# Modulation by quarters of the features, and six projections of layer one summed between them

## The chip, the cores and the metric

The kernel runs on one core of a Trainium2 chip. The metric is the device time of one execution in microseconds. Five engines work side by side and meet at semaphores: TensorE (matmuls into psum, which has eight banks of 128x512 fp32 here), VectorE, ACT (ScalarE), GpSimd (POOL) and SyncE (SP), which only issues transfers. All transfers of this kernel are issued by SP, in order, and are carried by 16 DMA engines.

## The reference

A block of two layers over 256 tokens and 256 context tokens with 1024 features, and behind it two more layers of another kind. Only the beginning of the first layer matters here:

```python
silu_c, silu_cc = jax.nn.silu(c), jax.nn.silu(c_ctx)
for l in range(DEPTH):
    mod = silu_c @ mod_w[l] + mod_b[l]          # 3 x 1024: shift, scale, gate
    mod_c = silu_cc @ mod_w[l] + mod_b[l]
    x, xc = trunk_layer(x, xc, mod, mod_c, ...)

# trunk_layer
shift, scale, gate = jnp.split(mod[:, None, :], 3, axis=-1)
z = split_columns((rmsnorm(x, pre_g) * (1 + scale) + shift) @ w_in)
zc = split_columns((rmsnorm(xc, pre_g) * (1 + scale_c) + shift_c) @ w_in)
```

The columns of z that appear below are mla_q (256, "q"), mla_kv (128, "kv"), mla_kr with the two small gate ranks ("misc"), pool_x and pool_gate (512 each, "px" and "pg"). q and kv are normalised and feed an attention of eight heads; px and pg feed a pooling branch; both end in a merge.

## The kernel before

**Tiles.** Activations lie with features on the partitions: xn holds the normalised, modulated input as 8 blocks of 128 features by 512 tokens (context in columns 0 to 255, x in 256 to 511). Each value is kept as two parts, h (rounded to float32r) and l (the rest), written by `split` (L382: a cast on ACT, a subtraction on VectorE). Weights come in chunks of 128x1024 fp32, loaded by `raw` (L357, the transfer is L361) and split by `W_` (L368: the cast L377 on ACT, the subtraction L379 on VectorE, or on GpSimd for every second chunk while `lopool[0]` is 2). `mm3` (L391) makes three float32r matmuls for each block of 128 features: h by h, h by l, l by h (L395 to L397). A product of one chunk with xn (`ws`, L399) is 8 blocks by 3, 24 matmuls into one bank. wp is the pool of the weights, with three raw buffers, three for h and three for l.

**The start (L1111 to L1144).** Four token tiles are loaded (L1117), with the constants and the vectors (L1119, L1121). Each is scaled by its reciprocal norm (L1128, L1129) and transposed by TensorE (L1133) into xT. `mod_cols` (L473) then computes shift and scale: for each of four groups of 512 columns `mod_rows` (L458) loads four chunks of the modulation weights and makes 16 small matmuls (L466, eight records in the trace for each chunk, 32 output rows at a time), copies the bank (L470), transposes it (L479), reduces it to columns (L482) and adds the bias (L483; L486 for the scale). The groups come in the order 0, 2, 1, 3: shift and scale of the first half of the features, then of the second. After each half, xT is scaled and shifted in place (L1142, two token groups for each of four blocks) and split into xn (L1144). The raw modulation chunks lie in a pool "bd" with 16 buffers, which also holds xT and is closed after the start.

**Layer one (L634, called from L1168).** `latents` (L644) makes the products q 0, q 1, kv and misc by `win` (L640), takes squares for their norms, splits the scaled latents, sums the squares by one-column matmuls (L669, L671), takes reciprocal roots on GpSimd, spreads them by transposes (L445, L680, L683) and multiplies two loaded tables by them (L687, L688). `mla` (L697) then makes the values (uv), keys (uk) and queries (uq) of the heads from the split latents; the first scores are L735. `poolb` (L978) makes px g and pg g for four groups g. `trunk_core` (L1088) weaves these generators: for each step of the attention, a fraction of a step of the pooling and merging branch, and 0.7 of a step of the second layer's modulation (`mod_cols(1, md1)`, L1169). The tiles of latents, mla and poolb come from a pool "mla0" (L1091) that is opened after "bd" is closed.

**The order.** The program order gives priorities; a scheduler with a time model writes each engine's instructions in a fixed order from them before the run. On the chip each engine keeps that order and waits at semaphores. `ahead[0]` gives weights a higher priority from the latents on. Psum banks have three tags: "mm" with three, "at" with three, "aux" with two (L299 to L306). A product or a transpose holds its bank until it has been read.

## Time and profile before

| what | us |
|---|---|
| median of three runs | 1570.56 (1567.63 to 1571.66) |
| the profiled execution, its own time | 1570.03 |
| its span | 1568.3 |
| TensorE busy in it | 1492.4 |
| VectorE, ACT, GpSimd busy | 949.9, 756.1, 360.9 |
| transfers | 229.79 MB |

The profile is of one execution. Busy time of TensorE is from modelled ends, so that a busy TensorE need not be at its peak. [...] In rows of the trace a line names the line of the code, which may be that of a helper; "xna" is the first half of xn, "xnb" the second; PEld is TensorE's loading of weights, which overlaps its matmuls.

### The profile page before, as it was taken

What the parts mean: (1) busy time and instruction counts of PE and PEld (TensorE: products, weight loads), DVE (VectorE), ACT (ScalarE), POOL (GpSimd) and SP (SyncE); (2) the same over time, 40 slices, a digit from 0 to 9 for tenths busy, and PEclk for the clock granted to TensorE, in tenths of its full rate; (3) what the DMA queues carried; (4) which work ended last, traced back from release to release, by engine and by line L of the source; (5) the groups of instructions that cost most, each with busy time, mean ns of one, the idle gap of its engine ahead of it and who ended that gap; (6) DMA issues with size and microseconds to landing.
All of it is one profiled execution on the core that took longest, in us unless ns stands there. A gap on an engine that the chain in (4) does not pass through costs nothing.

```text
span 1568.3 us, 25530 instructions
## 1 busy us (share of the span) xinstructions
PE 1492.4 (95%) x10206; PEld 1284.0 (82%) x10206; DVE 949.9 (61%) x1479; ACT 756.1 (48%) x1267; POOL 360.9 (23%) x276
## 2 busy tenths in 40 slices
PE   6999999999999999998989989989999997899998
PEld 3766668787877789777889989869999887799986
DVE  5555435856445576667694764767665577656654
ACT  4444344453323365755644454554444457534443
POOL 1213125735400002336582020311000034100000
PEclk9999999999999999999999999999999999899999
DMA  8323322222334465224337664425556654435564
GB/s 340 121 103 125 121 90 81 66 76 68 108 110 163 144 189 168 95 74 137 104 133 254 196 217 145 132 85 169 165 186 187 217 187 148 140 130 179 185 187 135
DMA packets 65638, 229.79 MB, mean 147 GB/s; under 512 B 7280, under 2 KB 7920, under 8 KB 65392
## 3 DMA queue, kind: packets, MB, share of 16 engines
q1 hardware_dynamic: 65520, 228.16, 44.9%
q8 instruction: 80, 1.31, 0.3%
q14 instruction: 38, 0.31, 0.1%
HBM read 227.09 MB, written 1.05 MB: 145 GB/s over the span
## 4 chain that ended last, share of the span: by engine, by line
PE 77%; DVE 7%; POOL 4%; issue 4%; DMA 4%; ACT 4%; SPq 0%; POOLq 0%; DVEq 0%; ACTq 0%
PE mm L395 21%; PE mm L397 21%; PE mm L396 21%; DMA wr<-in_w_dram 3%; PE at L735 2%; DVE wl L379 2%; PE aux L768 2%; ACT wh L377 1%; PE at L755 1%; POOL wl L379 1%; POOL E L915 1%; POOL qp L895 1%; PE mm L466 1%; PE at L859 1%; PE aux L466 1%
## 5 line engine op out<-in xcount | busy, mean ns | idle before, releaser
L377 ACT ACTIVATE wh<-wr 128x1024 fp32r<-128x1024 f32 x352 | 370.8, 1055 | 424.9 <-PE mm L396 133.5
L379 DVE TENSOR_TENSOR wl<-wr,wh 128x1024 fp32r<-128x1024 f32 x288 | 363.9, 1265 | 287.2 <-ACT wh L377 285.9
L395 PE MATMUL mm<-xnah,wh 128*128 128x256 f32 (+1 forms) x1192 | 367.9, 309 | 11.2 <-DVE rt L1452 10.3
L397 PE MATMUL mm<-xnah,wl 128*128 128x256 f32 (+1 forms) x1192 | 361.9, 304 | 3.0 <-DVE wl L379 2.1
L396 PE MATMUL mm<-xnal,wh 128*128 128x256 f32 (+1 forms) x1192 | 362.0, 304 | 0.2 <-DVE xnal L386 0.2
L395 PEld LDWEIGHTS mm<-xnah,wh 128*128 128x128 f32 x1192 | 226.6, 190 | 27.8 <-DVE rt L1452 10.6
L379 POOL TENSOR_TENSOR wl<-wr,wh 128x1024 fp32r<-128x1024 f32 (+1 forms) x64 | 158.3, 2473 | 353.3 <-ACT wh L377 268.8
L397 PEld LDWEIGHTS mm<-xnah,wl 128*128 128x128 f32 x1192 | 226.6, 190 | 14.9 <-DVE wl L379 2.7
L396 PEld LDWEIGHTS mm<-xnal,wh 128*128 128x128 f32 x1192 | 226.8, 190 | 10.1 <-issue 1.4
L419 POOL TENSOR_TENSOR sm<-sm,minus_half 128x1 f32<-128x1 f32 (+3 forms) x34 | 25.5, 751 | 628.7 <-DVE sm L567 356.3
L395 PE MATMUL mm<-xnbh,wh 128*128 128x512 f32 (+1 forms) x392 | 138.2, 353 | 0.0
L397 PE MATMUL mm<-xnbh,wl 128*128 128x512 f32 (+1 forms) x392 | 136.9, 350 | 0.0
L396 PE MATMUL mm<-xnbl,wh 128*128 128x512 f32 (+1 forms) x392 | 136.7, 349 | 0.0
L395 PE MATMUL mm<-wh,xnah 128*128 128x256 f32 x288 | 84.3, 294 | 8.5 <-ACT xnah L385 6.3
L395 PEld LDWEIGHTS mm<-xnbh,wh 128*128 128x128 f32 x392 | 75.6, 193 | 11.8 <-issue 2.5
L397 PEld LDWEIGHTS mm<-xnbh,wl 128*128 128x128 f32 x392 | 75.6, 193 | 11.2 <-issue 2.4
L396 PEld LDWEIGHTS mm<-xnbl,wh 128*128 128x128 f32 x392 | 75.7, 193 | 11.0 <-issue 2.1
L396 PE MATMUL mm<-wl,xnah 128*128 128x256 f32 x288 | 83.3, 291 | 1.1 <-POOL wl L379 1.1
L397 PE MATMUL mm<-wh,xnal 128*128 128x256 f32 x288 | 82.6, 290 | 0.7 <-DVE xnal L386 0.7
L396 PE MATMUL mm<-wl,hh 128*128 128x512 f32 x176 | 68.8, 391 | 0.0
L397 PE MATMUL mm<-wh,hl 128*128 128x512 f32 x176 | 68.8, 391 | 0.0
L395 PE MATMUL mm<-yh,wh 128*128 128x512 f32 (+1 forms) x192 | 65.6, 342 | 0.9 <-ACT scr L1030 0.9
(365 smaller groups left out, 2895.5 us busy)
## 6 DMA issues: line engine op xcount, KB each, us to landing
wr<-in_w_dram SPq DMA_DIRECT2D x398, 512.0 KB, 3.6
wr<-in_w_dram SPq DMA_DIRECT2D x18, 256.0 KB, 2.7
row<-in_rows_dram SPq DMA_DIRECT2D x8, 512.0 KB, 5.4
xt<-in_xin_dram SPq DMA_DIRECT2D x4, 512.0 KB, 5.8
scr<-in_rows_dram SPq DMA_DIRECT2D x8, 256.0 KB, 4.8
xr<-in_xin_dram SPq DMA_DIRECT2D x2, 512.0 KB, 4.7
xc<-in_xin_dram SPq DMA_DIRECT2D x2, 512.0 KB, 4.7
toep<-in_toep_dram SPq DMA_DIRECT2D x1, 1024.0 KB, 7.0
```

The source lines that it names most:

```text
L377: S.activation(ch.h, r, AF.Copy)
L379: eng.tensor_tensor(ch.l, r, ch.h.bitcast(F32), op=OP.subtract)
L395: T.matmul(dst, lh, rh, start=first and i == 0, stop=False)
L396: T.matmul(dst, lh, rl, start=False, stop=False)
L397: T.matmul(dst, ll, rh, start=False, stop=last and i == n - 1)
L419: G.tensor_tensor(y, m, minus_half[:, :n], op=OP.pow)
L466: T.matmul(p[32 * j:32 * j + 32, c0:c0 + 256], sc[:, k * 32:k * 32 + 32], r[:, j, :], start=half == 0, stop=half == 1, tile_position=(0, 3 ...
L735: T.matmul(pa[:, :n], qxs[pr, j][:, c0 + qt * P:c0 + qt * P + P], kxs[pr, j][:, :n], start=True, stop=True)
L755: T.transpose(pa[:, k * 256 + qt * P:k * 256 + qt * P + P], r[qt][:, (2 * k2 + k) * P:(2 * k2 + k + 1) * P], ident)
L768: T.matmul(py[64 * j:64 * j + 64, c0:c0 + 256], v[:, k, h * 64:h * 64 + 64], pTs[j][k // 2][:, k % 2, :], start=k == 0, stop=k == nk - 1, ...
L859: T.matmul(pa[c * s:c * s + s, t * 2 * s:(t + 1) * 2 * s], k_[:, i:i + s], q_[:, :, j:j + s], start=True, stop=True, tile_position=(0, c * s))
L895: (V, G)[j].tensor_tensor(b[r, j, :], gq[r], e[r], op=OP.mult)
```

## The change

`mod_cols` goes by quarters of the features: each of its four groups now holds 256 columns of the shift and the 256 of the scale that belong to them, so that after each group two blocks of features can be finished. It yields once more in each quarter. For the first layer its bank comes from "aux" and its raw chunks from 12 buffers.

In the start, the weights of six products (q 0, q 1 with the first quarter; kv, misc with the second; px 0, pg 0 with the third) are loaded behind the modulation chunks of that quarter, into the same 12 buffers, and split; h and l of the first three lie in wp, those of the last three in a new pool "early". After each quarter, its two blocks of xn are written and every product that has its weights takes the matmuls of these two blocks (and of all earlier blocks when it has just come). Each product has one bank that stays open from its first block to its last: three "mm", three "at". `win` later returns the finished bank instead of making the product. Transfers of weights from the latents on are queued on SP behind the last of these chunks until `begun[0]` is cleared.

```diff
+EARLY = [[("q", 0), ("q", 1)], [("kv", 0), ("misc", 0)], [("px", 0), ("pg", 0)], []]
+MODBUFS = 12
...
     def raw(key, pl=wp, bufs=3, width=CW):
...
-        nc.sync.dma_start(t[:, :n], w[INDEX[key]][:, :n])
+        with tc.issue_after(begun[0]) if begun[0] is not None else nullcontext():
+            begun[1] = nc.sync.dma_start(t[:, :n], w[INDEX[key]][:, :n])
...
-    def W_(key, pl, bufs):
-        r = raw(key)
+    def W_(key, pl, bufs, *where):
+        r = raw(key, *where)
...
-    def mod_rows(l, cb2, ptile, *where):
+    def mod_rows(l, cbs, ptile, *where):
+
         p = ptile()
-        for cb in (2 * cb2, 2 * cb2 + 1):
-            c0 = (cb % 2) * 256
+        for n, cb in enumerate(cbs):
+            c0 = n * 256
...
-    def mod_cols(l, md, *where):
-        md.col = const.tile([P, 16, 2], F32, name=f"mcol{l}")
-        for cb2 in (0, 2, 1, 3):
-            mr = yield from mod_rows(l, cb2, mmps, *where)
+    def mod_cols(l, md, ptile, *where):
+
+        col = const.tile([P, 4, 2, 2, 2], F32, name=f"mcol{l}")
+        md.shift = lambda kk, m: col[:, kk // 2, 0, kk % 2, m:m + 1]
+        md.scale = lambda kk, m: col[:, kk // 2, 1, kk % 2, m:m + 1]
+        for q in range(4):
+            mr = yield from mod_rows(l, (q, 4 + q), ptile, *where)
             pc = auxps()
             for j in range(4):
                 T.transpose(pc[:, j * P:(j + 1) * P], mr[:, j * P:(j + 1) * P], ident)
-            cl = md.col[:, 4 * cb2:4 * cb2 + 4, :]
-            bias = VC(("shift_b", l), 4 * cb2, 4) if cb2 < 2 else VC(("scale_b", l), 4 * cb2 - 8, 4)
+            cl = col[:, q].rearrange("p a k r -> p (a k) r")
             V.tensor_reduce(cl, pc.rearrange("p (j g r) -> p j r g", j=4, g=4)[:, :, 0:2, :], axis=AX.X, op=OP.add)
-            V.tensor_tensor(cl, cl, bias[:, :, None].to_broadcast([P, 4, 2]), op=OP.add)
-            if cb2 >= 2:
-                pre = VC(("pre", l), 4 * cb2 - 8, 4)
-                V.scalar_tensor_tensor(cl, cl, 1.0, pre[:, :, None].to_broadcast([P, 4, 2]), op0=OP.add, op1=OP.mult)
-        yield
+            for i, name in enumerate(("shift_b", "scale_b")):
+                bias = VC((name, l), 2 * q, 2)
+                V.tensor_tensor(col[:, q, i], col[:, q, i], bias[:, :, None].to_broadcast([P, 2, 2]), op=OP.add)
+            pre = VC(("pre", l), 2 * q, 2)
+            V.scalar_tensor_tensor(col[:, q, 1], col[:, q, 1], 1.0, pre[:, :, None].to_broadcast([P, 2, 2]), op0=OP.add, op1=OP.mult)
+            yield
...
         def win(name, i, t0=T0, t1=512):
+            if (name, i) in M.ready:
+                return M.ready.pop((name, i))[:, :t1 - t0]
             return ws(W(("win", l, name, i)), xn, t0, t1)
...
             weaves(M.latents(mp), (fill, 0.3))
+            begun[0] = None
...
-        mc = mod_cols(0, md0, bd, 16)
-        for half in range(2):
-            for _ in range(9 if half == 0 else 8):
+
+        ep = mkpool(st, "early")
+        mc = mod_cols(0, md0, auxps, bd, MODBUFS)
+        chs = []
+        for q in range(4):
+            for _ in range(5):
                 next(mc, None)
-            for k in range(4 * half, 4 * half + 4):
+            for key in EARLY[q]:
+                n = len(chs)
+                where = (wp if n < 3 else ep, 3)
+                ch = W_(("win", 0, *key), *where, bd, MODBUFS)
+                chs.append((key, ch, (mmps if n < 3 else atps)()))
+            for k in (2 * q, 2 * q + 1):
                 for g in range(2):
                     gs = slice(g * 256, g * 256 + 256)
...
+                    V.tensor_scalar(xT[:, k, gs], xT[:, k, gs], md0.scale(k, 1 - g), md0.shift(k, 1 - g), op0=OP.mult, op1=OP.add)
                 split(xn, (ALL, k), xT[:, k, :])
+            for key, ch, d in chs:
+                k0 = 0 if key in EARLY[q] else 2 * q
+                mm3(d, [(ch.h[:, k, :], ch.l[:, k, :], xn.h[:, k, :], xn.l[:, k, :]) for k in range(k0, 2 * q + 2)],
+                    k0 == 0, q == 3)
+        M0.ready.update({key: d for key, _, d in chs})
...
     trunk_layer(0, md0, xn, M0)
-    trunk_core(0, M0, mod_cols(1, md1))
+    begun[0] = begun[1].ins
+    trunk_core(0, M0, mod_cols(1, md1, mmps))
```

## Rows read from the trace of the kernel before

**Rows 1.** The page: busy us, share of the span, instructions of each engine.
```profile
PE 1492.4 (95%) x10206; PEld 1284.0 (82%) x10206; DVE 949.9 (61%) x1479; ACT 756.1 (48%) x1267; POOL 360.9 (23%) x276
```
**Rows 2.** Stretches: length, busy time by engine, granted clock, DMA share, GB/s.
```profile
12.00:20.30 8.30, 7.20 (x76) 4.01 (x68) 6.25 (x31) 4.08 (x9) 0.55 (x1) 1.00 1.02 409
20.30:28.00 7.70, 3.78 (x44) 1.21 (x44) 6.01 (x18) 2.52 (x4) 0.00 (x0) 0.99 1.03 407
28.00:32.00 4.00, 3.84 (x32) 1.46 (x36) 1.64 (x5) 0.00 (x0) 0.00 (x0) 0.60 1.03 410
32.00:41.00 9.00, 7.28 (x36) 4.85 (x29) 7.67 (x14) 5.66 (x7) 2.40 (x1) 1.00 0.48 161
...
58.00:62.00 4.00, 4.00 (x12) 3.10 (x12) 0.83 (x3) 0.27 (x1) 2.00 (x2) 0.57 0.49 150
...
77.60:157.00 79.40, 79.40 (x405) 54.75 (x401) 44.77 (x98) 35.90 (x76) 17.93 (x14) 1.00 0.33 113
```
**Rows 3.** In order of time, TensorE: start, length, instruction, idle before and releaser.
```profile
16.47 1.07 PE L466 MATMUL mm<-wr,sc 128*32 128x256 f32 x16
...
21.65 0.64 PE L466 MATMUL mm<-wr,sc 128*32 128x256 f32 x8 [0.64 <-DMA wr<-in_w_dram]
...
31.80 0.16 PEld L466 LDWEIGHTS mm<-wr,sc 128*32 128x32 f32 x8 [0.36 <-DMA wr<-in_w_dram]
...
33.25 0.66 PE L479 MATMUL aux<-ct,scr 128*128 128x128 f32 x4 [0.81 <-DVE scr L470]
```
**Rows 4.** In order of time: the chain from the modulation to the first products.
```profile
23.54 2.67 DVE L1142 TENSOR_SCALAR xT<-xT,mcol 128x256 f32<-128x256 f32 x8
...
32.51 0.69 DVE L470 COPY scr<-mm 128x512 f32<-128x512 f32 x1 [0.73 <-PE mm L466]
...
35.45 2.40 POOL L379 TENSOR_TENSOR wl<-wr,wh 128x1024 fp32r<-128x1024 f32 x1 [21.14 <-ACT wh L377]
...
35.59 4.68 DVE L1142 TENSOR_SCALAR xT<-xT,mcol 128x256 f32<-128x256 f32 x8
...
39.10 0.50 PE L395 MATMUL mm<-xnbh,wh 128*128 128x512 f32 x1
```
**Rows 5.** The tile xT: scalings, ns at least/median/most.
```profile
L1142 DVE TENSOR_SCALAR xT<-xT,mcol x16: 400/406/2409, 23.5 to 39.9; 128x256 f32<-128x256 f32 x16
```
**Rows 6.** In order of time: cast and subtraction of a weight chunk.
```profile
33.06 1.06 ACT L377 ACTIVATE wh<-wr 128x1024 fp32r<-128x1024 f32 x1 [6.18 <-DMA wr<-in_w_dram]
...
34.26 1.22 DVE L379 TENSOR_TENSOR wl<-wr,wh 128x1024 fp32r<-128x1024 f32 x1
```
**Rows 7.** In order of time, TensorE: matmuls of a product; first one on latents.
```profile
48.34 0.39 PE L396 MATMUL mm<-xnal,wh 128*128 128x512 f32 x1
48.58 0.40 PE L397 MATMUL mm<-xnah,wl 128*128 128x512 f32 x1
...
69.42 0.39 PE L395 MATMUL mm<-wh,kvnh 128*128 128x512 f32 x1
```
**Rows 8.** In order of time, TensorE: the norms' small matmuls, and the first scores.
```profile
54.19 1.62 PE L669 MATMUL aux<-ct,scr 128*128 128x1 f32 x14
...
56.87 1.05 PE L671 MATMUL aux<-ct,scr 128*128 128x1 f32 x8 [0.49 <-ACT scr L661]
...
66.20 1.03 PE L445 MATMUL aux<-ct,sm 128*128 128x128 f32 x8
...
77.55 1.13 PE L735 MATMUL at<-kx,qx 128*128 128x256 f32 x4
```
**Rows 9.** The last splits of xT, and what waited for them (last row: SP's waits).
```profile
41.32 2.49 DVE L386 TENSOR_TENSOR xnbl<-xT,xnbh 128x512 fp32r<-128x512 f32 x4
...
43.89 0.63 ACT L385 ACTIVATE pwh<-wr 128x512 fp32r<-128x512 f32 x1 [2.96 <-DVE xnbl L386]
...
44.56 0.69 DVE L386 TENSOR_TENSOR pwl<-wr,pwh 128x512 fp32r<-128x512 f32 x1 [0.75 <-ACT pwh L385]
...
SPq L687 <- DVE xnbl L386: 2.0, 1, 2.0
```

More of the change, by code (lines that the diff above doesn't have):

```diff
@@ L1 @@
-from contextlib import ExitStack
+from contextlib import ExitStack, nullcontext
 import numpy as np
@@ L355, in trunk_and_stack @@
     lopool = [0]
+    begun = [None, None]
     def raw(key, pl=wp, bufs=3, width=CW):
@@ L493, in mod_gates @@
         for c in range(2):
-            mr = yield from mod_rows(l, 4 + c, auxps, *where)
+            mr = yield from mod_rows(l, (8 + 2 * c, 9 + 2 * c), auxps, *where)
             bB, pB = rowhalf(("mod_b", l), c), rowhalf(("post", l), c)
@@ L536, in prenorm_trunk @@
                 sl = slice(k * 256, k * 256 + 256)
-                scale, shift = md.col[:, 8 + kk, m:m + 1], md.col[:, kk, m:m + 1]
+                scale, shift = md.scale(kk, m), md.shift(kk, m)
                 if k == 0:
@@ L1107, in trunk_and_stack @@
     md0, md1, M0, M1 = Obj(), Obj(), Obj(), Obj()
+    M0.ready, M1.ready = {}, {}
     right = ctx.enter_context(ExitStack())
@@ L1134, in trunk_and_stack @@
                 S.activation(xT[:, 4 * k4:4 * k4 + 4, t * P:t * P + P], p.rearrange("p (k t) -> p k t", k=4), AF.Copy)
-        mc = mod_cols(0, md0, bd, 16)
-        for half in range(2):
-            for _ in range(9 if half == 0 else 8):
-                next(mc, None)
-            for k in range(4 * half, 4 * half + 4):
+        ep = mkpool(st, "early")
[3 more added lines that the diff above has]
+            for _ in range(5):
+                next(mc, None)
+            for key in EARLY[q]:
[4 more added lines that the diff above has]
+            for k in (2 * q, 2 * q + 1):
                 for g in range(2):
                     gs = slice(g * 256, g * 256 + 256)
-                    V.tensor_scalar(xT[:, k, gs], xT[:, k, gs], md0.col[:, 8 + k, 1 - g:2 - g], md0.col[:, k, 1 - g:2 - g],
-                                    op0=OP.mult, op1=OP.add)
+                    V.tensor_scalar(xT[:, k, gs], xT[:, k, gs], md0.scale(k, 1 - g), md0.shift(k, 1 - g), op0=OP.mult, op1=OP.add)
                 split(xn, (ALL, k), xT[:, k, :])
+            for key, ch, d in chs:
[3 more added lines that the diff above has]
+        M0.ready.update({key: d for key, _, d in chs})
     lam = VC("lam")
```

## The prediction, made before the changed kernel was run

> **What bounds the kernel now.** I read the page's row of engines, then the stretches of the beginning with busy time and granted clock, then the beginning in order of time. TensorE is busy for 95% of the span [rows 1], and from 77.60 to 157 it is busy for 79.40 of 79.40 us at full clock [rows 2]: in that stretch there is no idle time to fill, so what TensorE does earlier shortens it. Idle time is left at the start. [...] Over that whole start the transfers run at 407 to 410 GB/s with the DMA engines full [rows 2]. So the start is bound by transfers: a chunk of 128x1024 fp32 (0.524 MB) takes 0.524/407 = 1.28 us, TensorE needs 0.64 us for its eight matmul records, and the last of the sixteen chunks of shift and scale is in at 31.80 [rows 3]. Behind that stands a fixed chain before a product can use the new features: the copy, four transposes (0.66 us), the reduction and biases, eight scalings, the splits [rows 3, 4].
>
> **The DMA order.** Six chunks of the first layer's weights (q 0, q 1, kv, misc, px 0, pg 0) move in front of the last modulation chunk. No byte is added. Counted back from 31.80, chunk slot n is in at 31.80 - 1.28 x (16 - n). The last modulation chunk of quarter 1 is slot 4 (16.4), of quarter 2 slot 10 (24.1), of quarter 3 slot 16 (31.8), of quarter 4 slot 22 (39.5): the modulation ends 7.7 us later than before. Fewer buffers (12 for 16) cost nothing by this order, as slot 13 reuses what slot 1 filled some 15 us earlier; without that cover one chunk of 1.28 us would be late.
>
> **The chain of a quarter.** Before, the second half took 39.10 - 31.80 = 7.3 us from its last chunk to the first product on the new features [rows 3, 4]. Its eight scalings took 4.68 us where those of the first half took 2.67, because one of them lasted 2.41 us beside GpSimd's subtraction of 2.40 us [rows 4, 5]. In the changed part the six subtractions are all on VectorE (the counter that gives every second one to GpSimd is still 0), so that those 2.0 us go. I take 5.0 us a quarter (bounds: 4 and 7.3), so new features are there at 21.4, 29.1, 36.8 and 44.5. VectorE has the load for it: four chains of some 4.0 us (0.7 copy, 4 scalings at 2.67/8, two splits at 2.49/4, and 0.7 as an estimate for four small ones [rows 4, 9]), six subtractions of 1.22 us [rows 6] and the small operations, at most the 6.25 us that it was busy from 12.00 to 20.30 [rows 2], are 30 us in the 32 us from 12 to 44: full, but in front. ACT's six more casts of 1.06 us [rows 6] have more room still. One more bias operation in each quarter is 0.2 us of its chain, inside the 5.0.
>
> **TensorE.** A product's matmul takes 0.235 us in a stream (48.34 to 48.58) [rows 7]; a product has 24, so 5.6 us, six 33.8. By quarters they are 12, 36, 60 and 36 matmuls: 2.8, 8.5, 14.1 and 8.5 us. A quarter of modulation is four chunks at 1.07/2 us [rows 3] and the transposes, 2.8 us. Quarter 1 of the products runs from 21.4 to 24.2 and then waits for features until 29.1. From there TensorE has work in hand: 29.1 + 8.5 + 2.8 = 40.4, + 14.1 + 2.8 = 57.3, + 8.5 = 65.8. At 65.8 all six products are closed. Before, five of them and 3.7 us of small matmuls (1.62 + 1.05 + 1.03) [rows 8] were done when the first product on the normalised latents started at 69.42 [rows 7]. Six products without the small ones would have been done at 69.42 - 3.7 + 5.6 = 71.3. The gross gain is **5.5 us**.
>
> **What is given back: the pool.** The tiles of the attention stage lie in a pool on the memory of the start's pools. Before, the first write to it on ACT and the first load into it on SP both waited until the last split of xT ended at 43.8, though they have nothing to do with xT [rows 9]: a pool is handed over when its last user is done. The change puts a second pool there, for the weights of misc, px 0 and pg 0, whose last reader is the last matmul of pg 0, at 65.8. So the split latents, the tables and the pool weights wait for that end, where before they were written from 43.9 on. After it come three casts on ACT (0.63 each) and one subtraction (0.69) [rows 9] before a latents product can start, 2.7 us with gaps. Part of the 3.7 us of small matmuls, whose inputs lie elsewhere, fills it. Bounds 0 and 2.7 us; I take **1.5**. Two of the three raw buffers (pool weights, uk) stay taken until then too, and SP's queue stands behind them; the uv weights have the third and come through, so I cost that at nothing. If uv were queued behind, its transfer and casts, 1.28 + 1.06 + 1.22 = 3.6 us at the least [rows 6], would be bare.
>
> **The clock.** The lower level came in 28 to 32 after a stretch with TensorE half idle, and again in 58 to 62 in a stretch of one-column matmuls [rows 2, 8]. The first cost little then, as TensorE waited for chunks; now products would run in it. The second cost 4 x 0.43 = 1.7 us. The new start may lose 1.7 us at 29 and be spared those at 58, or have both. Bounds -1.7 and +1.7; I take **0.8** lost.
> [...]
>
> **Psum and later work.** The six open sums hold six banks (three "mm", three "at") until read; the transposes of x use "at" too, but come before all of them. The first score matmul comes at 77.55 [rows 8], later than any of the six is read but pg 0's; if that one stayed, the scores would have two banks for three. I cost it at nothing, at most 2 us. The second layer's modulation has the same matmuls, one operation more per quarter on engines that are not the bound, and three of its twenty steps now come after the attention stage: nothing, at most 0.5 us. The order the scheduler writes for the rest of layer one can shift by a microsecond or two either way.
>
> **Sum.** 5.5 - 1.5 - 0.8 = 3.2 us less. The profiled execution took 1570.03 us (span 1568.3), so 1566.8; the median of the runs, 1570.56, stands 0.5 above it. I predict **1567.0**. About 0.3% (4.7 us) is what a measurement here tells from no change, so the forecast itself is in "the same".
>
> **Rivals.**
> First, *the whole gain*: the small matmuls cover the pool's hand-over, and the denser TensorE stream is spared the low clock at 58. Then 5.5 to 7.2 us go: 1570.0 - 6.4 = 1563.6. For it: 3.7 us of cover against 2.7 of chain. Against it: the first writers all waited for the pool in the trace [rows 9].
> Second, *the score chain sets the pace*, and it ends slower. pg 0 moves in front of the latents, so the scores come later: 65.8 + 3.7 + 1.5, then 8.1 us from the first latents product to the first scores as before (69.42 to 77.55) [rows 7, 8], is 79.1, 1.6 us later. TensorE gets its 5.6 us back only if the attention stage is bound by TensorE. If it is bound by its own chain, the delay stays: 1.6, with the 0.8 of the clock and up to 3.6 for weights that wait behind the pool, 1572 to 1576; 1574.5 as one value. It decides when the first scores come after 82. Against it: 79.40 of 79.40 us busy [rows 2]; but a busy TensorE in this profile is not one at its peak.
> [...]
> Fourth, *the products do not come between*: TensorE's queue is in order, and if it holds the open sums behind later modulation chunks they start at 39.5 + 0.6 and end at 40.1 + 33.8 = 73.9 instead of 71.3, slower by 2.6 and the pool's 1.5: 1574.1. Before, products and modulation chunks were hardly mixed, so the trace says little.
>
> **How the numbers follow.** The forecast (0.44) and the third rival (0.10) are within 0.3%, but for some 0.08 of the forecast's spread beyond 1565.9; the whole gain has 0.29; the score chain 0.11, of which 0.03 stays within; the products not between 0.06, half within. That is faster 0.37, the same 0.52, slower 0.11; as the order of all of layer one is written anew, and the bounds of the small items lean to loss, I move 0.05 from the same to slower. Range 1561.5 to 1574.5: from the whole gain with a little more to the slower rivals' values.
>
> **What would show it.** Right: the last modulation matmul near 39.5; products of q 0 by 22; TensorE busy from 29 to 66 nearly without a break; pg 0's last matmul at 64 to 69; then ACT's and VectorE's splits waiting for that matmul, and latents products 1 to 3 us behind. Wrong: splits of the latents written before pg 0 ends (no hand-over, whole gain); TensorE idle by 3 us or more between 29 and 60 waiting for modulation chunks (fourth rival); first scores after 82, or idle TensorE in the attention stage (second); a clock of 0.5 in 21 to 33 (third).

## The result, and the profile after

The changed kernel takes **1578.24 us** (median of 11 runs, 1573.73 to 1582.66) where the kernel before takes 1569.78 in the same session (11 runs, 1565.77 to 1573.29): a ratio of **1.0057**, 95% interval 1.0042 to 1.0072. It is slower by 0.57%. The forecast was 1567.0 with a range to 1574.5, so the prediction fell on the wrong side. The profiled execution took 1573.86 us (span 1571.9), at the low end of its runs. The ratios leave out a single slow execution, one of the twelve of e11, which took 2930.69 us.

The page's row of engines first, the counterpart of [rows 1]:

```profile
PE 1491.0 (95%) x10206; PEld 1281.9 (82%) x10206; DVE 955.5 (61%) x1494; ACT 755.7 (48%) x1267; POOL 352.1 (22%) x273
```

As many matmuls, and TensorE's busy time the same within 0.1%. So nothing was added to the bound engine: it stands idle, or works at the lower clock, somewhere that it did not before. The stretches of the changed kernel show where (columns as in [rows 2]: length, busy time by engine, granted clock, DMA share, GB/s). The granted clock is a share of full speed; read in slices of 0.5 us it is 1.00 or 0.50 all through 12 to 90, in both kernels, but for the slices in which it changes:

```profile
12.00:20.30 8.30, 6.04 (x63) 3.24 (x55) 6.46 (x27) 5.72 (x11) 0.54 (x1) 0.99 1.03 410
20.30:28.00 7.70, 5.98 (x26) 3.15 (x27) 6.98 (x19) 3.33 (x4) 0.00 (x0) 0.56 1.03 408
28.00:32.00 4.00, 4.00 (x23) 2.67 (x22) 0.69 (x1) 0.00 (x0) 0.00 (x0) 1.00 1.03 409
32.00:41.00 9.00, 8.68 (x66) 6.32 (x64) 8.01 (x22) 3.90 (x6) 0.00 (x0) 1.00 0.85 333
41.00:62.00 21.00, 18.01 (x98) 13.01 (x97) 4.33 (x12) 1.58 (x3) 0.00 (x0) 0.98 0.00 1
62.00:77.00 15.00, 14.29 (x65) 11.86 (x64) 8.24 (x17) 7.35 (x14) 3.26 (x5) 0.84 0.38 106
77.00:157.00 80.00, 77.75 (x387) 51.83 (x387) 48.46 (x96) 39.29 (x80) 17.03 (x16) 0.99 0.36 116
```

Up to 41 TensorE is filled as was foreseen (busy for 18.7 us of 20.7 in 20.30 to 41, where before it was 14.9), and the transfers are over at 41. But TensorE is then idle for 3.0 us in 41 to 62, for 0.7 in 62 to 77 and for 2.2 behind 77. The same stretches of the kernel before had next to no idle time:

```profile
41.00:62.00 21.00, 20.51 (x95) 16.60 (x94) 10.59 (x16) 6.91 (x11) 5.82 (x6) 0.92 0.52 163
62.00:77.00 15.00, 15.00 (x74) 11.64 (x76) 6.03 (x11) 8.90 (x14) 3.43 (x2) 1.00 0.22 72
77.00:157.00 80.00, 80.00 (x413) 54.93 (x405) 45.37 (x99) 36.50 (x77) 18.09 (x16) 1.00 0.33 112
```

In order of time, all engines of the changed kernel (columns: start, length, engine, line, instruction; in brackets the idle time before it and what released it):

```profile
55.89 1.93 PE L474 MATMUL aux<-wr,sc 128*32 128x256 f32 x30
57.87 0.69 DVE L478 COPY scr<-aux 128x512 f32<-128x512 f32 x1 [15.76 <-PE aux L474]
...
58.62 0.66 PE L490 MATMUL aux<-ct,scr 128*128 128x128 f32 x4 [0.81 <-DVE scr L478]
...
60.01 1.38 DVE L1165 TENSOR_SCALAR xT<-xT,mcol 128x256 f32<-128x256 f32 x4
60.78 1.27 ACT L392 ACTIVATE xnbh<-xT 128x512 fp32r<-128x512 f32 x2 [19.40 <-DVE xT L1165]
...
61.46 1.65 PE L402 MATMUL mm<-xnbh,wh 128*128 128x512 f32 x3 [2.19 <-ACT xnbh L392]
...
71.17 0.39 PE L404 MATMUL at<-xnbh,wl 128*128 128x512 f32 x1
...
71.60 1.15 ACT L392 ACTIVATE qnh<-scr 128x512 fp32r<-128x512 f32 x2 [0.55 <-PE at L404]
71.62 0.11 POOL L999 MEMSET u<- 128x16 f32 x1 [57.42 <-PE at L404]
...
74.84 0.79 PE L402 MATMUL mm<-wh,kvnh 128*128 128x512 f32 x1 [0.71 <-ACT kvnh L392]
...
76.51 2.37 POOL L386 TENSOR_TENSOR wl<-wr,wh 128x1024 fp32r<-128x1024 f32 x1
76.53 2.90 DVE L1017 SCALAR_TENSOR_TENSOR scr<-us,u 128x512 f32<-128x512 f32 x1
...
80.36 1.09 PE L452 MATMUL aux<-ct,sm 128*128 128x128 f32 x8 [1.61 <-POOL sm L426]
```

Read it from the top. The last quarter's modulation matmuls (30 of 32 records) run in one burst at 55.89, though no transfer has run since 41: their data had lain there for some 15 us (VectorE's copy had been waiting for 15.76). What stood in front of them in TensorE's queue were 56 matmuls of products, from 42.57 on, nearly all of the third quarter. The chain of the last quarter (copy, transposes, scalings, split) then stands bare: from 57.82 to 61.46, 3.64 us, TensorE has only 0.66 us of transposes to do. It comes back at the lower clock (0.68 in 62 to 66), and the last early product, pg 0, closes at 71.56, where 65.8 was forecast. There the hand-over of the pool waits, as foreseen: ACT, GpSimd (idle for 57.42 us) and SP's load of a table are all released by pg 0's last matmul. The first product on the latents starts at 74.84 [rows 7: 69.42], the first scores at 89.3 [rows 8: 77.55].

The scalings of xT lost their outlier, as foreseen (ns at least, median, most; before in [rows 5], with one of 2409):

```profile
L1165 DVE TENSOR_SCALAR xT<-xT,mcol x16: 406/410/414, 21.6 to 61.0; 128x256 f32<-128x256 f32 x16
```

Not all of the 11.8 us by which the scores come later is loss: pg 0 (5.6), one modulation chunk of the second layer (0.5) and a small product (0.7) now stand in front of them, so some 5 us are. Most of these come late. At the first product on the latents the change is only 0.8 us behind (74.84 against 69.42 + 5.6 for pg 0 - 1.0 for small transposes that now stand behind it): up to there the bare chain has used up the gain and no more. Behind it TensorE works at a low clock, and then waits 1.61 us at 80.36; before, it was busy all the time, at full clock:

```profile
74.80:78.80 4.00, 3.90 (x9) 2.79 (x9) 3.96 (x7) 1.42 (x2) 4.00 (x3) 0.57 0.89 255
```

```profile
69.40:77.50 8.10, 8.10 (x46) 5.69 (x44) 3.42 (x7) 7.26 (x12) 3.58 (x4) 1.00 0.19 68
```

But the kernel falls back further. Scores, and the first matmuls of the next stage ("blocks", L859 before, L872 after), first and last start, before and after:

```profile
L735 PE MATMUL at<-kx,qx x64: 377/538/697, 77.6 to 214.2; 128*128 128x256 f32 x32, 128*128 128x512 f32 x32
L859 PE MATMUL at<-qp,gk x64: 218/219/243, 251.2 to 356.1; 128*32 128x64 f32 x64
```

```profile
L748 PE MATMUL at<-kx,qx x64: 377/536/697, 89.3 to 216.2; 128*128 128x256 f32 x32, 128*128 128x512 f32 x32
L872 PE MATMUL at<-qp,gk x64: 219/219/243, 260.3 to 365.9; 128*32 128x64 f32 x64
```

The last scores are only 2.0 later (214.2 and 216.2), the blocks 9.1: 7 of these arise **between the last scores and the blocks**, where the prediction had put nothing. The span of the profiled execution is only 3.6 us longer because behind 262 it happened to lose 13.0 us to the lower clock (length times one minus the granted clock, over stretches of 2 us) where the execution before lost 19.3; over all versions that sum runs from 13.0 to 21.7, so that a single span says little about the start.

### The profile page after: what moved, and what is told of

Same layout as the page of the kernel before. It is cut to its first block, busy times and chain, and to the rows that moved or that the text cites. A ratio compares the mean times of both kernels' runs of the same rounds, so it can differ in the third digit from the quotient of the medians.

```text
span 1571.9 us, 25541 instructions
## 1 busy us (share of the span) xinstructions
PE 1491.0 (95%) x10206; PEld 1281.9 (82%) x10206; DVE 955.5 (61%) x1494; ACT 755.7 (48%) x1267; POOL 352.1 (22%) x273
## 4 chain that ended last, share of the span: by engine, by line
PE 75%; DVE 10%; ACT 5%; issue 4%; DMA 4%; POOL 3%; POOLq 0%; DVEq 0%; SPq 0%; ACTq 0%
PE mm L402 20%; PE mm L403 20%; PE mm L404 20%; DMA wr<-in_w_dram 3%; DVE wl L386 3%; PE at L748 2%; ACT wh L384 2%; PE aux L781 2%; PE at L768 1%; PE aux L474 1%; POOL wl L386 1%; POOL E L928 1%; POOL qp L908 1%; PE at L872 1%; DVE E L925 1%
## 5 line engine op out<-in xcount | busy, mean ns | idle before, releaser
L384 ACT ACTIVATE wh<-wr 128x1024 fp32r<-128x1024 f32 (+1 forms) x352 | 370.6, 1055 | 412.4 <-issue 133.3
L402 PE MATMUL mm<-xnah,wh 128*128 128x256 f32 (+1 forms) x1180 | 363.4, 309 | 16.2 <-DVE rt L1480 10.4
L404 PE MATMUL mm<-xnah,wl 128*128 128x256 f32 (+1 forms) x1180 | 357.7, 303 | 1.7 <-DVE wl L386 1.5
L403 PE MATMUL mm<-xnal,wh 128*128 128x256 f32 (+1 forms) x1180 | 357.7, 303 | 0.0
L386 POOL TENSOR_TENSOR wl<-wr,wh 128x1024 fp32r<-128x1024 f32 x61 | 150.5, 2468 | 282.4 <-ACT wh L384 244.6
L402 PE MATMUL mm<-xnbh,wh 128*128 128x256 f32 (+1 forms) x380 | 131.8, 349 | 2.2 <-ACT xnbh L392 2.2
L403 PE MATMUL mm<-xnbl,wh 128*128 128x512 f32 (+1 forms) x380 | 130.5, 344 | 0.0
L404 PE MATMUL mm<-xnbh,wl 128*128 128x256 f32 (+1 forms) x380 | 129.8, 342 | 0.0
L403 PEld LDWEIGHTS mm<-xnbl,wh 128*128 128x128 f32 x380 | 71.6, 189 | 10.3 <-issue 2.2
L404 PEld LDWEIGHTS mm<-xnbh,wl 128*128 128x128 f32 x380 | 71.6, 189 | 10.3 <-issue 2.0
```

The costliest lines, as they stand in the source:

```text
L384: S.activation(ch.h, r, AF.Copy)
L386: eng.tensor_tensor(ch.l, r, ch.h.bitcast(F32), op=OP.subtract)
L402: T.matmul(dst, lh, rh, start=first and i == 0, stop=False)
L403: T.matmul(dst, lh, rl, start=False, stop=False)
L404: T.matmul(dst, ll, rh, start=False, stop=last and i == n - 1)
```

## The experiments

Four explanations stood after the profile. **The order of the queue**: products stand in front of the last quarter's modulation. **The hand-over**: the pool "early" holds up the attention stage's first writes. **The steps**: the second layer's modulation now yields 20 times, not 17, so that at 0.7 of a step per step of the attention three chunks are left when the attention is over. **The clock**: early products run at a lower clock (0.56 in 20.30 to 28, 0.68 in 62 to 66), and TensorE loses more by it than before. e10 to e15 add matmuls whose results are overwritten, and leave nothing out.

**e1, the order.** The products of a quarter are written behind the modulation of the next one; the last ones behind the loop.

```diff
+        def products(q):
+            for key, ch, d in chs:
+                if any(key in e for e in EARLY[:q + 1]):
...
         for q in range(4):
...
                 split(xn, (ALL, k), xT[:, k, :])
-            for key, ch, d in chs:
-                k0 = 0 if key in EARLY[q] else 2 * q
...
+            if q:
+                products(q - 1)
+        products(3)
```

> Edit: in program order the products of a quarter are written behind the modulation and the xn of the next quarter, so that these have the higher priority. Theory A (the last quarter's modulation matmuls stood on TensorE's queue behind the products of the third quarter, 55.9 us instead of about 41, so that its chain was bare): the last modulation matmul comes before 48 us, TensorE is not idle for 3.0 us at 58 to 61.5, the matmul that closes pg 0 ends at 66.5 to 68 instead of 71.6, and the time is 3 to 5 us below the changed kernel's. Rival B (the pool's hand-over behind pg 0 is what costs, and only its length counts): pg 0 closes earlier, but the first scores come no more than 1 us earlier and the time stays within 1.5 us of the changed kernel's. Rival C (the low clock): the granted clock in 20 to 28 and 74 to 78 stays at its lower level and the time gains under 2 us.

Measured: ratio 1.0035 (1.0020 to 1.0051). TensorE in order of time:

```profile
44.19 1.93 PE L474 MATMUL aux<-wr,sc 128*32 128x256 f32 x30
...
66.28 0.40 PE L404 MATMUL at<-xnbh,wl 128*128 128x512 f32 x1
66.51 1.84 PE L682 MATMUL aux<-ct,scr 128*128 128x1 f32 x16
...
74.87 1.97 PE L452 MATMUL aux<-ct,sm 128*128 128x128 f32 x8 [1.18 <-POOL sm L426]
```

The modulation runs 11.7 us earlier, the wait at 61.46 is gone, pg 0 closes at 66.7 and the first scores come at 84.6 instead of 89.3. So the order of the queue did what was said of it, and 65.8 was a fair figure for a queue in the right order. But the first blocks come only 2.0 us earlier (258.3), and the interval of the ratio still overlaps the change's (1.0042 to 1.0072).

**e2, the hand-over**, and **e3, both.** The pool "early" is opened below "bd", so that nothing of the attention stage lies on it.

```diff
+        ep = mkpool(st, "early")
         bd = mkpool(st, "bd")
...
-        ep = mkpool(st, "early")
         mc = mod_cols(0, md0, auxps, bd, MODBUFS)
```

> Edit: the pool for h and l of misc, px 0 and pg 0 is opened before the pool of xT, so that it lies under layer one's long-lived tiles and no longer under the attention stage's. Theory B (the hand-over costs): the splits of the latents start as soon as each product closes, some before pg 0's last matmul; the first product on latents follows pg 0 without idle time and the first scores come 2 to 4 us earlier than the 89.3 of the changed kernel; time 2 to 4 us below it. Rival A: the start up to 71.6 is unchanged and the small matmuls fill the gap anyway, so the scores come under 1 us earlier and the time stays within 1.5 us.

> Both edits. If A and B are two separate costs, the gains add: pg 0 closes at 66.5 to 68, the first scores at 82 to 84, and the time is 5 to 8 us below the changed kernel's, level with the kernel before or up to 3 us below it. If one of the two is only hidden by the other, the gain is that of the larger one, 3 to 5 us.

Measured: e2 1.0049 (1.0031 to 1.0067), e3 1.0021 (1.0007 to 1.0035). In e2 the casts that waited for pg 0 run at 60.90 and 61.44, while pg 0 closes at 69.5, and the first scores come at 85.5, 3.8 us earlier; yet the ratio moves by less than its interval. Some 2.0 of the 3.8 us are not the pool's: pg 0 itself closes 2.0 us earlier in this execution, which kept its full clock where the change's lost it (see the end). With the order repaired as well, e3 stands 0.0036 below the change, and the two intervals do not overlap: the two causes together are 5 to 6 us of the 8.5. Its first scores come at 84.0, 0.6 before e1's, and level with the kernel before when pg 0, the chunk and the small product are counted. In e3 a wait is left that the next experiments use:

```profile
73.48 1.19 PE L452 MATMUL aux<-ct,sm 128*128 128x128 f32 x8 [2.02 <-POOL sm L426]
```

The transposes that spread the latents' norms wait 2.0 us for GpSimd's reciprocal roots. Before, the products of px 0 lay there and covered it; now they are done.

**e4, the quarters alone**, without an early product.

```diff
-EARLY = [[("q", 0), ("q", 1)], [("kv", 0), ("misc", 0)], [("px", 0), ("pg", 0)], []]
+EARLY = [[], [], [], []]
```

> Edit: no product is started early (the list of early products is empty); modulation in quarters, twelve buffers, and the order on SP stay. If the open sums and the memory they need are what costs (A or B): time within 2 us of the kernel before. If the modulation by quarters itself costs (four chains instead of two, on the banks of the small tag): the products start 2 us or more later than the 34.2 of the kernel before, and the time is 3 us or more above it.

Measured: 1.0015 (1.0001 to 1.0030), 2.4 us and so between the two expectations; the first product starts at 34.07. Its start is better than before's (first scores 76.4 for 77.55), but its first blocks come at 255.1 for 251.2. TensorE behind the attention, in order of time:

```profile
222.45 1.06 PE L474 MATMUL mm<-wr,sc 128*32 128x256 f32 x12
...
225.31 1.06 PE L474 MATMUL mm<-wr,sc 128*32 128x256 f32 x12
...
230.72 0.51 PE L402 MATMUL mm<-xnah,wh 128*128 128x512 f32 x1 [2.00 <-ACT wh L384]
...
232.61 0.50 PE L402 MATMUL mm<-xnah,wh 128*128 128x512 f32 x1 [1.16 <-ACT wh L384]
```

Three chunks of the second layer's modulation (x12 and x12: 24 of the 128 records) are left for the end, and behind them the next products wait for weights that have been cast too late. The changed kernel has the same two waits, at 235.93 and 237.82 (2.07 and 1.16 us), with a clock of 0.93 and 0.90 in 230 to 250.

**e5, e6, e8, the steps.** In the second layer the modulation yields once at its end, as before: 17 steps. e5 is the change with that, e6 is e3 with that, e8 is e4 with that.

```diff
-            yield
+            if l == 0 or q == 3:
+                yield
```

> Edit: the second layer's modulation yields once at its end, as before the change, and not once more in each quarter: 17 steps, not 20; the first layer's start is that of the changed kernel. Theory D (the three steps that came after the attention stage put three chunks of modulation weights in front of the weights of the next stage, which cost the 7 us between the last scores and the first gated-attention blocks): the modulation's last matmuls of that layer come before the last weighted sums, TensorE does not wait for a weight cast around 230, first blocks less last scores is 37 to 39 us as in the kernel before (44 in the changed kernel), and the time is 4 to 7 us below the changed kernel's. Rival E (that stretch is longer because the start left another order, whatever the steps): it stays 42 to 45 us and the time within 1.5 us of the changed kernel's.

> Edit: 17 steps, modulation before the products in program order, and the pool of the open sums under the long-lived tiles. If A, B and D add: 4 to 7 us below the run with the first two edits alone (ratio 1.0021), so 1566 to 1569, 1 to 4 us below the kernel before. If E holds: no change against that run.

> Edit: no product started early, 17 steps. Modulation by quarters alone. If D is right the 2.4 us (ratio 1.0015) that the run without early products was above the kernel before go: ratio 0.997 to 1.0005. If quarters themselves cost: ratio stays at 1.001 to 1.002.

Measured: e5 1.0048 (1.0028 to 1.0068), e6 1.0011 (0.9995 to 1.0027), e8 0.9991 (0.9971 to 1.0010). All three have no idle time in 230 to 250, and from the last first-layer scores to the first blocks it takes 37.0 to 37.1 us, as before (251.2 - 214.2 = 37.0), where the six kernels with 20 steps (the change, e1 to e4, e14) take 44 to 45. That shows the mechanism. Its worth is smaller than those 7 us, since with 17 steps the chunks stand among the scores: the last scores of e5 come at 221.0 (216.2 in the change). Net, the first blocks come earlier by 2.3 (change to e5), 3.1 (e3 to e6) and 6.2 us (e4 to e8); the ratios fall by 0.0009, 0.0010 and 0.0024, each by less than the two intervals are wide, all to the same side. e5 and e6 miss the times that were expected of them (4 to 7 us below the change, and below the kernel before); e8 meets its range.

**e7, four early products** (px 0 and pg 0 left where they were before), on top of e6.

```diff
-EARLY = [[("q", 0), ("q", 1)], [("kv", 0), ("misc", 0)], [("px", 0), ("pg", 0)], []]
+EARLY = [[("q", 0), ("q", 1)], [("kv", 0), ("misc", 0)], [], []]
```

> Edit: as the run before in this group, but only q 0, q 1, kv and misc are started early; px 0 and pg 0 come at their old place. Theory F (with all six done at once nothing is left to cover the latents' norms: TensorE is idle for 2 us and then at its lower clock around 71 to 78): the two products stand behind the norms' small matmuls, no wait for the reciprocal roots, first scores at 78 to 81, and the time 1 to 4 us below the run with six. Rival G (TensorE idles as much in the start when it has two products less to run): the idle time between 20 and 60 grows by 2 us or more and the time is within 1 us of the run with six, or above it.

Measured: 0.9996 (0.9980 to 1.0012), first scores 77.3, first blocks 250.1. The transposes of the norms don't wait; px 0's products lie in front of them again:

```profile
69.58 1.03 PE L452 MATMUL aux<-ct,sm 128*128 128x128 f32 x8
```

They did not wait in e6 either. There TensorE ran at half its clock at that place, so that the products filled the time; from the sums of the squares to the transposes it took 6.9 us in e3 (66.53 to 73.48) and in e6 (67.65 to 74.56). e6, TensorE, and its stretch of 70 to 76:

```profile
74.56 1.97 PE L452 MATMUL aux<-ct,sm 128*128 128x128 f32 x8
```

```profile
70.00:76.00 6.00, 6.00 (x20) 4.80 (x20) 3.59 (x9) 3.53 (x6) 3.23 (x4) 0.50 0.28 89
```

Rival G's idle time came as well: e7 is idle for 2.8 us in 42 to 90 and e6 not at all. Most of it stands in front of the last quarter's first product, whose transposes stand behind products again:

```profile
48.39 0.60 PE L490 MATMUL aux<-ct,scr 128*128 128x128 f32 x4
...
51.16 0.97 PE L402 MATMUL mm<-xnbh,wh 128*128 128x512 f32 x3 [1.71 <-ACT xnbh L392]
```

With order, pool and steps repaired the early sums are level with the kernel before, and with e8, which has none. **e9** takes misc out too and does without the pool "early":

> As e7_four_early, but with three early products (q 0, q 1, kv), whose split weights all lie in the pool of the weights, so that the pool 'early' is gone; the second layer's modulation keeps its 17 steps. If a second pool under the latents still costs e7 something: ratio 0.997 to 0.9985, first scores 76 or earlier. Rival, the early sums are worth nothing whatever their number, since what they fill at the start comes back as idle time and lower clock behind 42: ratio 0.9985 to 1.0005, first scores 76 to 78.

Measured: 1.0010 (0.9994 to 1.0025), first scores 79.2, later than either expectation, and a ratio above both, though its interval reaches into the rival's. So it is not the second pool that takes the gain, and fewer sums don't gain more.

**Where the gain of the early sums went** can be added up: TensorE's idle time, and its time lost to the clock (length times one minus the granted clock), over stretches of 2 us of the profiled executions.

| kernel | 12 to 42: idle, clock | 42 to 90: idle, clock | sum |
|---|---|---|---|
| before | 6.9, 1.7 | 0.5, 1.7 | 10.8 |
| changed | 4.3, 3.4 | 5.6, 3.4 | 16.7 |
| e7, four early | 4.5, 3.4 | 2.8, 1.7 | 12.4 |
| e8, none early | 8.5, 1.7 | 0.0, 0.0 | 10.2 |
| e10, four early, kept busy | 1.0, 0.0 | 2.6, 1.7 | 5.3 |

The open sums fill 2.4 us of the start's idle time in e7 (6.9 to 4.5), and the lower clock and new gaps take it back. Idle time at the lower clock counts in both columns, so the sums are rough. The last row belongs to the next experiment; to its 5.3 belong some 4.4 us of added matmuls (an estimate from four groups of 1.03 to 1.13 us), together 9.7, 2.7 less than e7, where the first blocks differ by 1.4.

**e10, the clock.** e7 with two matmuls on each second modulation chunk of quarters one and two (8 in all), whose results the next matmul overwrites, so that TensorE works while it waits for chunks.

```diff
                 r = raw(("mod", l, cb, half), *where)
+                if l == 0 and cbs[0] < 2 and half == 0:
+                    for _ in range(2):
+                        T.matmul(p[:, c0:c0 + 256], ones, r[:, 0, :], start=True, stop=True)
```

> As e7_four_early, with two more 128x128 by 256 matmuls on each of the first four modulation chunk pairs (quarters one and two), whose results are overwritten at once: TensorE works while it waits for chunks. If the lower clock in 20.30 to 28 (0.59 in e7, so 3.1 us of the 7.70) is what takes back the early sums' gain: clock over 0.9 in that stretch, first scores 1.5 to 3 us before e7's 77.3, ratio 0.9975 to 0.999. Rival, the clock costs nothing there because TensorE waits for chunks in that stretch at either level: clock over 0.9, but first scores within 0.7 us of 77.3 and the ratio within 0.001 of e7's 0.9996. Second rival: the clock stays under 0.7 although TensorE is busy.

Measured: **0.9975** (0.9958 to 0.9991). One stretch of e7, and the same of e10:

```profile
20.30:28.00 7.70, 5.93 (x27) 3.15 (x28) 7.04 (x19) 3.33 (x4) 0.00 (x0) 0.59 1.03 409
```

```profile
12.00:20.30 8.30, 7.48 (x56) 3.81 (x54) 6.18 (x26) 5.95 (x11) 0.55 (x1) 1.00 1.03 411
20.30:28.00 7.70, 7.48 (x55) 4.58 (x56) 6.63 (x20) 3.23 (x4) 0.00 (x0) 1.00 1.03 408
```

Busy for 7.48 of 7.70 us, TensorE shows a granted clock of 1.00 (0.59 in e7). The first product on the last quarter's features runs at 49.18 (51.16 in e7), the first blocks come at 248.7 (250.1), the span is 1564.1 (1566.7). The first scores come at 79.9, against the expectation, but with 20 more matmuls of products in front of them (4.7 us); less these they would stand 2.1 us before e7's. The clock is not all that changed. In e10 the last quarter's transposes run in front of nearly all of the third quarter's products, and its first product does not wait; in e7 they ran at 48.39, and the wait was 1.71 us:

```profile
44.07 0.60 PE L493 MATMUL aux<-ct,scr 128*128 128x128 f32 x4
...
49.18 0.87 PE L402 MATMUL mm<-xnbh,wh 128*128 128x512 f32 x3
```

So up to 1.7 of the 2.0 us can be the scheduler's new order.

**e11 to e13, is it the clock alone?** The same matmuls added (12 here, in the last three groups) to the kernel before (e11) and to the quarters without early products (e12), and e10's kernel once more beside them (e13).

> The kernel before, with two more matmuls of 128x128 by 256 on every second modulation chunk of the last three groups, overwritten at once. If the clock alone is the gain of e10: clock over 0.9 in 28 to 32, first scores 1 to 2 us before 77.55, ratio 0.9975 to 0.999. If the gain needs the early sums: ratio 0.999 to 1.001, since TensorE waits for chunks until 31.8 and after it loses at most the 1.6 us of low clock in 28 to 32, and most of that stands beside the wait for chunks.

> As e8_quarters_steps17 (no early product), with the added matmuls in the last three quarters. If the clock alone is the gain of e10: ratio 0.997 to 0.9985. If the sums are what gains under a full clock: within 0.001 of e8's 0.9991, and above e10 by 0.001 or more in this call.

> The same kernel as e10_kept_busy, beside the other two. 0.9960 to 0.9990 again; if the sums are what gains, at least 0.001 below both.

Measured, in one session: e11 1.0014 (1.0000 to 1.0029), e12 1.0015 (0.9999 to 1.0031), e13 **0.9970** (0.9956 to 0.9984). e11 in the stretch that ran at 0.60 before:

```profile
28.00:32.00 4.00, 4.00 (x35) 2.10 (x39) 1.83 (x5) 0.00 (x0) 0.00 (x0) 1.00 1.03 411
```

The full clock came back there and bought nothing, as there is nothing but modulation chunks to work on; the first scores come at 77.4 as before. e12 is a poorer control: its first product waits for a subtraction of a weight.

```profile
39.12 0.79 PE L404 MATMUL mm<-xnah,wl 128*128 128x512 f32 x1 [3.39 <-DVE wl L386]
```

Against the kernel before, full clock without the sums gains nothing (e11), sums without the full clock gain nothing (e7, e9), both together gain 0.25 to 0.30%, twice. Two things stay open. The added matmuls also change the order that the scheduler writes, and the clock and that order were not told apart. And the sums were not told apart from the quarters: e8, without sums and without added matmuls, has its first blocks at 248.9, as early as e10 (248.7) and e13 (248.8), and its interval (0.9971 to 1.0010) overlaps theirs. That the sums are worth anything beyond the quarters stands on ratios from different sessions alone; the one control for it in e13's session is e12.

**e14 and e15**, the added matmuls of e10 in the changed kernel as it was, and in e6 (all six early; order, pool and steps repaired).

> The changed kernel with the matmuls of e10 added in quarters one and two, nothing else. If the lower clock is the first cause of its 0.57%: ratio 1.001 to 1.003, first scores 86 to 87.5 (after: 89.3). If order, pool and steps are the cause and the clock only adds to them: ratio 1.0035 to 1.0055.

> e6_both_steps17 (all six early, order and pool repaired, 17 steps) with the same added matmuls; e6 was 1.0011. If the lack of cover at the latents' norms costs the last two sums their gain: ratio 0.9975 to 0.9995, above e13's 0.997. Rival, under a full clock six gain more than four: 0.995 to 0.9965.

Measured: e14 1.0068 (1.0049 to 1.0086), e15 0.9997 (0.9982 to 1.0013). e14, TensorE in order of time:

```profile
46.27 1.93 PE L477 MATMUL aux<-wr,sc 128*32 128x256 f32 x32
...
57.00 0.27 PE L493 MATMUL aux<-ct,scr 128*128 128x128 f32 x1
...
59.46 1.14 PE L402 MATMUL mm<-xnbh,wh 128*128 128x512 f32 x3 [2.18 <-ACT xnbh L392]
```

Its clock is 1.00 from 12 to 52, its modulation runs at 46.27, but the last transpose stands behind products until 57.00 and the bare wait of 2.2 us is as long as ever. So the lower clock of the start was not the first cause of the loss; e14 leaves order, pool and steps as they were and keeps the loss. It came out above its expectation even for that case (1.0035 to 1.0055), though its interval reaches into it. What the clock costs behind the bare wait e14 doesn't say: there it lost 6.8 us in 42 to 90 by the sum of the table above, the change 3.4 there and 3.4 in the start.

e15 has its first blocks at 249.9, 2.9 us before e6, in which TensorE had no idle time left behind 42: so the added matmuls help where no wait like e7's is there to be taken away. The ratio, a little above its expected range, does not settle it. e15 stands above e13, as the lack of cover would have it, but it ran in another session and the two intervals just overlap: whether the sixth and fifth sum cost anything under a full clock stays open.

**All versions side by side.** In front of the first blocks TensorE has the same matmuls in every version (but for the added ones), so that this time compares the starts. It is of one execution each, and the clock alone can move it by nearly 2 us (1.7 us between e2 and the changed kernel, see the end).

| version | first blocks, us | ratio to the kernel before |
|---|---|---|
| before | 251.2 | |
| changed | 260.3 | 1.0057 |
| e1, order | 258.3 | 1.0035 |
| e2, pool | 257.7 | 1.0049 |
| e3, order and pool | 255.9 | 1.0021 |
| e4, no early product | 255.1 | 1.0015 |
| e5, 17 steps | 258.0 | 1.0048 |
| e6, e3 with 17 steps | 252.8 | 1.0011 |
| e7, e6 with four early | 250.1 | 0.9996 |
| e8, e4 with 17 steps | 248.9 | 0.9991 |
| e9, three early | 252.8 | 1.0010 |
| e10 and e13, e7 kept busy | 248.7, 248.8 | 0.9975, 0.9970 |
| e11, before, kept busy | 251.0 | 1.0014 |
| e12, e8 kept busy | 254.7 | 1.0015 |
| e14, changed, kept busy | 262.1 | 1.0068 |
| e15, e6 kept busy | 249.9 | 0.9997 |

## Why the prediction was wrong

**The DMA order** held: all transfers of the start are over by 41. **The chain of a quarter** held for the last one alone: the long scaling is gone, and from the end of the last modulation matmul to the first product it took 3.64 us, inside what 5.0 from the last chunk allowed. In the first quarter it took 6.3 us (16.77 to 23.08), since two subtractions of weights, 1.22 us each, stood between its steps on VectorE.

**The TensorE step failed first.** It let every modulation matmul run when its chunk came and added products in the time between (29.1 + 8.5 + 2.8 = 40.4). In the kernel the last quarter's modulation stood behind products, at 55.89, and its chain ran bare; pg 0 closed at 71.56, so that of the gross gain of 5.5 us (65.8 against 71.3) nothing was left. It began in the second quarter, where it cost nothing yet: its transposes stood behind products until 32.06, and its features were used at 34.85, not 29.1. The fourth rival had named the mechanism, TensorE's queue in order, but the other way round (products held behind chunks) and with a chance of 0.06; the price it gave, 1574.1, is nearer than the forecast. With the order repaired, pg 0 closed at 66.7 for the 65.8 forecast: the arithmetic of that step was good, its premise on the order was not.
TensorE kept to the order of its queue (matmuls with data since 41 start at 55.89, behind 56 matmuls of products), and that order is one a scheduler wrote, from priorities in which a quarter's products stand ahead of the next quarter's modulation.

**The pool** came as forecast in kind: ACT, GpSimd and SP waited for pg 0's last matmul. Its size can be bounded alone only poorly: by the ratios 0.0008 (e2) and, with the order right, 0.0014 (e1 to e3), that is 1.3 to 2.2 us, for 1.5 taken; neither is clear of the intervals. What the step did not see is that the two moved products had been **cover** for the norms' chain: 1.61 us of wait in the change, 2.0 in e3, none in e7. How much that is worth is not shown: e6, against which e7 has the ratio lower by 0.0015, had no wait there but the lower clock, and the intervals overlap.

**The clock** was under-sized. Bounds were -1.7 and +1.7 us; the profiled execution lost 6.8 us to it up to 90, where before it lost 3.4. The third rival's sign, a clock of 0.5 in 21 to 33, came: half of the loss lies there (0.56 in 20.30 to 28), and half behind the bare wait (0.68 in 62 to 66, 0.57 in 74.80 to 78.80). That the first half was not the first cause is shown by e14; that the clock decides whether the open sums pay is what e10 to e13 suggest, with the order as a rival.
With the added matmuls the clock stayed at 1.00 through the waits for chunks (12 to 42 in e11 and e13), and the ratio fell only where other work behind the wait was there to be done (0.9970 in e13, 1.0014 in e11).

**"Psum and later work" failed second.** "Three of its twenty steps now come after the attention stage: nothing, at most 0.5 us" turned out as 2.3 to 6.2 us at the first blocks. The matmuls themselves are 2.1 us (two rows of 1.06), moved and not added; what was missed is that their transfers, and the weights queued behind them, come late for the products that follow (2.07 and 1.16 us of wait) and that the clock falls with it (0.93 and 0.90 in 230 to 240 and 240 to 250, 1.00 before).

**The second rival's** sign, first scores after 82, came true (89.3), but not its mechanism. In the change the last scores are only 2.0 us later, partly because three chunks had moved behind them; in e5, with 17 steps as before, they are 6.8 us later (221.0 and 214.2) of 11.7 at the first scores, with no idle time of TensorE in 90 to 215. So the stage was bound by TensorE and not by its own chain: pg 0's time came back, the time lost in front of the scores did not.

By ratios, the 0.57% divide as follows: order and hand-over 0.36 (e3), steps 0.10 (e6), px 0 and pg 0 left where they were 0.15 (e7), which leaves nothing. By the first blocks, the 9.1 us divide into 2.0 for the order, 2.4 for the hand-over, 3.1 and 2.7, which is 1.1 more than all. By the ratios the first term and the sum stand outside their intervals; the split of the last two does not.

## What to carry to other kernels

When a change puts new work between old work on an engine with one queue, look up which of the two has the higher priority where both are ready: filler with the higher priority held up the chain that feeds the next filler here (modulation at 55.89 in the changed kernel, 44.19 in e1). Work moved forward was also cover where it lay, and a generator that yields more often is finished later by whoever paces it: count both. Filling the gaps of a start bound by transfers (408 to 410 GB/s from 12 to 32) did not pay by itself: the four early sums beat the kernel before (0.9975 and 0.9970) only with eight matmuls that compute nothing of use, through which TensorE kept its full clock (1.00 in 20.30 to 28, where e7 shows 0.59). Whether that is the clock, the order that came with them, or mostly the quarters, was not told apart: compare such a version with one that has only the cheaper half of the change (here e8), in one session.

## What the runs showed of the hardware that was not expected

**The same start can run at either clock.** Up to 40, e2 has the same matmuls in the same order in TensorE's queue as the changed kernel. Its profiled execution waited longer for the first product (2.07 us, 1.72 in the changed kernel) and still held the full clock where the change's fell to 0.56:

```profile
20.30:28.00 7.70, 5.63 (x40) 3.12 (x33) 7.20 (x20) 3.34 (x4) 0.00 (x0) 1.00 1.03 409
```

From the first product to the first matmul into an "at" bank it took 5.84 us in e2 (22.83 to 28.67) and 7.58 in the changed kernel (23.08 to 30.66): 1.7 us. With the same queue, e2 was 2.0 us ahead at the end of pg 0 (69.5 and 71.6). e1, e3, e5, e6, e7 and e9 showed 0.56 to 0.78 there. So the clock of such a stretch can differ between nearly equal starts, and one profile alone doesn't price it.

**VectorE beside GpSimd.** The instruction at 76.53 took 2.90 us next to GpSimd's subtraction of 2.37, where it takes 0.68 at 103.98, with GpSimd idle; the scaling of 2409 ns in [rows 5] was stretched in the same way beside a subtraction of 2.40. ACT waited 3.24 us for it; TensorE's wait at 80.36 was for another, a reciprocal root that stood behind that subtraction in GpSimd's queue. The change removed one such pair and the new order made another.
